# The first splits of the mixed outputs queued in pairs behind attention units, the mask put into the decays, and a query tile with pages of its own

## The chip, the cores and the metric

The kernel runs on one core of a Trainium2 chip. The metric is device time in microseconds of one execution, as the median of several runs. A profile is one execution with every instruction recorded; its span goes from the first to the last instruction. Engines: PE (TensorE matmuls), PEld (its weight loads), DVE (VectorE), ACT (ScalarE), POOL (GpSimd), SP (the queue that issues most DMAs).

## The reference

One encoder layer on a sequence of 1024 with width 1024. Both mixers read the same normalised input; their outputs are joined, projected and added, and a feed-forward layer follows.

```python
def reference(x, ...):
    u = rms_norm(h, mix_norm_gain)
    aq, ak, av, dqkv, dgate, da, db = split(u @ w_in)
    o_att = rms_norm(chunked_rel_attention(aq, ak, av, ...), att_out_gain)  # 8 heads of 64, 576 keys a chunk
    dq, dk, dv = split(silu(causal_short_conv(dqkv)))
    o_dn = gated_delta_rule(dq, dk, dv, log_decay, beta)                    # 4 heads of 128, chunks in turn
    o_dn = rms_norm(o_dn, dn_out_gain) * silu(dgate)
    h = h + concat([o_att, o_dn]) @ w_out
    z = rms_norm(h, ffn_norm_gain) @ w_ff1
    return h + square(relu(z)) @ w_ff2
# in gated_delta_rule, for each chunk:
    l_mask = where(tril, exp(where(tril, diff, 0.0)), 0.0)       # diff: differences of summed log decays
    attn_intra = where(tril, (q @ k.T) * l_mask, 0.0)
```

## The kernel before, in words

All matrix products of the projections are exact to nearly float32: each operand is split into a high part (a cast to a shorter float32 form, by ACT, line 142) and a low part (the difference, by DVE or POOL, line 145), and three products are summed (`mm3`, line 158).

The stages, in order of time: the projections of the input (to about 347 us), then attention and the delta rule together (to about 584 us), then the output projection (to about 676 us), then the feed-forward layer to the end.

Attention works in units (`attention`, line 698): two groups `g` of four heads, eight tiles `t` of 128 queries, two pairs `pp` of heads, 32 units in all. `start` loads a tile's query page by two DMAs on SP, 64 partitions each (line 760), into one of two pages "x", which the tiles use in turn; high and low part of the queries are the two halves (`m`) of the page. `score` makes the products (lines 778 and 779), adds a bias and takes a minimum on DVE (lines 794 and 803; the bias pages `biasn` of the first group lie in the two pages "on") and the exponential on ACT (lines 809 and 812). `value` transposes the result on PE (lines 830 and 841), copies it out of PSUM (`t_tb` by ACT, line 833; `t_ta` of the first head of the pair by ACT, line 846, of the second by DVE, line 844) and multiplies it with the values (line 851). Units of a tile `t` below 2 have no `t_ta`, so there are 24 such copies on each engine. `finish` and `turn` scale the tile, take the sum of its squares on ACT (line 879) and write it transposed into `mixa`.

The delta rule goes over eight chunks of 128 rows (`delta_all`, line 679). `delta_state` carries the state; `delta_out`, one chunk later, forms the decays `Lt` (`decay`, line 462: two POOL products, two matmuls, an exponential on ACT), multiplies the scores with them on DVE (line 654), masks the product on POOL (line 655), multiplies it with the new values on PE (`c_po`), adds, takes a sum of squares (`sumsq`), turns it into a factor by a row of small POOL instructions (`c_ss`, `c_v`, `c_y`, `c_t`, `c_r`) and scales the output with it on POOL (line 664). `delta_fin` transposes the output (`c_tpo`) and writes it into `mixd`.

`out_proj` (line 917) splits the mixed outputs of each half of the rows (`mixed(hf)`, line 929) into `mh` and `ml`, eight parts each, and multiplies them with the output weights (`op`). Only the first half's `mixed(0)` is under an order constraint (line 969).

The order in which each engine issues its instructions is fixed when the program is built: a planner goes through a simulated time with costs of its own, and takes on each engine the earliest written of the instructions that are then ready and have a page free. On the chip each engine issues in that order, and an instruction that must wait holds up those behind it. `tc.issue_after(ins)` puts what is written inside it, as far as it runs on the engine of `ins`, behind `ins` in that engine's order; it makes nothing wait for `ins` to end.

Of the kernel before, what the change touches and what calls it, by code (L numbers as in the profile page):

```python
# [8 lines left out]
F32 = mybir.dt.float32  # L9
F32R = mybir.dt.float32r  # L10
AF = mybir.ActivationFunctionType
ALU = mybir.AluOpType
AX = mybir.AxisListType

P = 128
SEQ = 1024
DM = 1024
# [17 lines left out]
N_W = 10  # L35
ORDER = "OSMOSMFSOMOSMSL"
LATE = 2
RS = "a"
NV = 6
WV = 2.5  # L40
# [3 lines left out]
def hymba_kernel(  # L44
# [20 lines left out]
    nc = tc.nc  # L65
# [16 lines left out]
    def page(tag, name, dt=F32, w=512):  # L82
        return pools[tag].tile([P, w], dt, tag=tag, name=name, bufs=slots[tag])
# [8 lines left out]
    def part(t, i):  # L92
        return t[:, i * 512:(i + 1) * 512]
# [7 lines left out]
    def b4(ap):  # L101
        return ap.rearrange("p (a b) -> p a b", a=4)
# [3 lines left out]
    tri_u = mpool.tile([P, P], F32, name="tri_u")  # L106
# [3 lines left out]
    for t, pat, cm, base in ((tri_u, 1, -1, 0), (tri_s, -1, 1, -1)):  # L110
        nc.gpsimd.affine_select(
            out=t, in_=ones, pattern=[[pat, P]], compare_op=ALU.is_ge,
# [27 lines left out]
    def split(src, hi, lo, hi_eng, lo_eng):  # L140
        if hi_eng is nc.scalar:
            nc.scalar.copy(hi, src)  # L142
        else:
            hi_eng.tensor_copy(hi, src)
        lo_eng.tensor_tensor(lo, src, hi.bitcast(F32), ALU.subtract)  # L145
# [79 lines left out]
    q_dr = dram.tile([NT, 64, 2, 2, 512], F32, name="q_dr")  # L225
# [218 lines left out]
    def bc_mask(m):  # L444
        return m.unsqueeze(1).broadcast_to([P, 4, P])

    def bc_row(s):
        return s.unsqueeze(2).broadcast_to([P, 4, P])
# [13 lines left out]
    def decay(tag, n, ab, h4, msk, lhs, eng):  # L462

        g1 = page(tag, n + "g1", F32R)
        g2 = page(tag, n + "g2", F32R)
        eng.tensor_tensor(b4(g1), bc_mask(msk), bc_row(ab["gh"][:, h4]), ALU.mult)
        nc.gpsimd.tensor_tensor(b4(g2), bc_mask(msk), bc_row(ab["gl"][:, h4]), ALU.mult)
        dp = bank(ps_d, n + "d")
        nc.tensor.matmul(dp, lhs, g1, start=True, stop=False)
        nc.tensor.matmul(dp, lhs, g2, start=False, stop=True)  # L470
        L = page(tag, n)
        nc.scalar.activation(L, dp, AF.Exp)
        return L

    last_delta = [None]

    def sumsq(sq, st, tp, n):
        last_delta[0] = nc.scalar.activation(sq, tp, AF.Square).ins
        ss = small(st, n + "_ss", 4)
        nc.vector.tensor_reduce(ss, b4(sq), AX.X, ALU.add)  # L480
        return ss
# [153 lines left out]
    def delta_out(c, ab, kTs, D):  # L635
        n = f"c{c}"
        T = "wh" if c + 1 < NT else "cv"
        h4 = slice(4 * c, 4 * c + 4)
        kT = kTs[c]
        dq, dg, vn, o = D.pop(c)  # L640
        Lt = decay(T, n + "_Lt", ab, h4, tri_u, tri_sr, nc.gpsimd)
        yield 450
        tp = bank(ps_d, n + "_tpq")
        four_t(tp, head(dq))
        nq = rsqrt("c", sumsq(tp, "c", tp, n + "q"), 4, 1.0, EPS, n + "q")
        qs = small("c", n + "_qs", 4)
        nc.gpsimd.tensor_scalar(qs, nq, P ** -0.5, None, ALU.mult)
        q2 = small("c", n + "_q2", 4)
        nc.gpsimd.tensor_tensor(q2, qs, qs, ALU.mult)
        yield 500  # L650
        mp = bank(ps_d, n + "_mt")
        four(mp, lambda h, hs: kT[:, hs], lambda h, hs: dq[:, hs])
        att = page(T, n + "_att")
        nc.vector.tensor_tensor(att, mp, Lt, ALU.mult)
        nc.gpsimd.tensor_tensor(b4(att), b4(att), bc_mask(tri_u), ALU.mult)
        yield 900
        po = bank(ps_d, n + "_po")
        four(po, lambda h, hs: att[:, hs], lambda h, hs: vn[:, hs])
        nc.vector.tensor_tensor(o, o, po, ALU.add)
        ss = sumsq(po, "c", o, n)  # L660
        nc.gpsimd.tensor_tensor(ss, ss, q2, ALU.mult)
        f = rsqrt("c", ss, 4, 1.0 / P, EPS, n)
        nc.gpsimd.tensor_tensor(f, f, qs, ALU.mult)
        nc.gpsimd.tensor_tensor(b4(o), b4(o), bc_row(f), ALU.mult)
        D[c] = o, dg
        yield 900

# [30 lines left out]
    def attention(after):  # L698
# [54 lines left out]
        def start(g, t):  # L753
            n = f"t{g}{t}"
            T = dict(n=n, k0=max(0, t - 4))
            T["kb"] = max(0, t - 1)
            q = page("x", n + "_q", F32R, w=DM)
            qf = q.bitcast(F32)
            for r0 in (0, 64):
                nc.sync.dma_start(out=qf[r0:r0 + 64].rearrange("p (m c) -> p m c", m=2), in_=q_dr[t, :, :, g, :])  # L760
            T["q"] = q
            T["sums"] = small("t", n + "_sum", 8)
            T["nm"] = small("t", n + "_nm", 8)
            T["s"] = {}
            tiles[g, t] = T

        def product(g, T, i, bk, off, ka, kb):

            q = T["q"]
            cost = 0  # L770
            for hf in range(2):
                a, b = max(ka, 4 * hf), min(kb, 4 * hf + 4)
                if a >= b:
                    continue
                k = keys[g][hf][i]
                o = bk[:, off + (a - ka) * P:off + (b - ka) * P]
                c = slice((a - 4 * hf) * P, (b - 4 * hf) * P)
                nc.tensor.matmul(o, q[:, i * P:(i + 1) * P], k[:, c], start=True, stop=False)  # L778
                nc.tensor.matmul(o, q[:, 512 + i * P:512 + (i + 1) * P], k[:, c], start=False, stop=True)  # L779
                cost += max(214, (b - a) * 107)  # L780
            return cost

# [34 lines left out]
        def value(g, t, pp):  # L817
            T = tiles[g, t]
            n, k0, kb = (T[k] for k in ("n", "k0", "kb"))
            na, nb = kb - k0, t + 1 - kb  # L820
            if pp == 0:
                T["po"] = bank(ps_o, n + "_o")
            po = T["po"]
            sa, sb = T["s"].pop(pp)
            T["spare"] = sb
            tp = bank(ps_t, f"{n}_tpb{pp}")
            for e in range(2):
                for j in range(nb):
                    c = e * 256 + 256 - (nb - j) * P
                    nc.tensor.transpose(tp[:, c:c + P], sb[:, c:c + P], ident)  # L830
            tb = page("raw", f"{n}_tb{pp}", w=516)
            w3 = [t_[:, 0:512].rearrange("p (a b) -> p a b", a=2)[:, :, 256 - nb * P:256] for t_ in (tb, tp)]
            nc.scalar.copy(*w3)
            ta = [None, None]
            if na:
                for e in range(2):
                    i = 2 * pp + e
                    tp = bank(ps_t, f"{n}_tpa{i}")
                    for j in range(na):
                        js = slice(j * P, (j + 1) * P)  # L840
                        nc.tensor.transpose(tp[:, js], sa[e][:, js], ident)  # L841
                    ta[e] = page("u", f"{n}_ta{i}")
                    if e:
                        nc.vector.tensor_copy(ta[e][:, 0:na * P], tp[:, 0:na * P])  # L844
                    else:
                        nc.scalar.copy(ta[e][:, 0:na * P], tp[:, 0:na * P])
            for j in range(na + nb):
                for e in range(2):
                    h = 4 * g + 2 * pp + e
                    c = j * P if j < na else e * 256 + 256 - (na + nb - j) * P  # L850
                    nc.tensor.matmul(po[64 * e:64 * e + 64, pp * P:(pp + 1) * P], vt[k0 + j][:, 64 * h:64 * h + 64],  # L851
                                     (ta[e] if j < na else tb)[:, c:c + P], start=(j == 0), stop=(j == na + nb - 1))
            return (na + nb) * 650
# [42 lines left out]
        for i in range(len(units) + lag + late):  # L896
            if i < len(units):
                g, t, pp = units[i]
# [8 lines left out]
            if lag <= i < len(units) + lag:  # L907
                g, t, pp = units[i - lag]
# [3 lines left out]
            if i >= lag + late:  # L912
                g, t, pp = units[i - lag - late]
# [3 lines left out]
    def out_proj():  # L917


        order = (4, 5, 6, 7, 0, 1, 2, 3)  # L920
        w, parts, R = [], [], {}
# [7 lines left out]
        def mixed(hf):  # L929
            parts.append([None] * NKT)  # L930
            low = [quarter(f"ml1{b}", F32R) for b in range(2)] if hf else None
            for k in order:
                src = part(mix[hf][k // 4], k % 4)
                hi = page("u" if hf else ("pp", "cv")[k // 4], f"mh{hf}{k}", F32R)
                lo = part(low[k // 4], k % 4) if hf else page("dk", f"ml{hf}{k}", F32R)
                split(src, hi, lo, nc.scalar, nc.vector)
                parts[hf][k] = hi, lo

        def rows(j, hf, acc):
# [26 lines left out]
            nc.sync.dma_start(out=r2_dr[:, hf * TH:(hf + 1) * TH], in_=acc)  # L966

        weights(0)
        with tc.issue_after(last_delta[0]):
            mixed(0)  # L970
        acc = rows(0, 0, None)
        weights(1)
        acc = rows(1, 0, acc)
# [376 lines left out]
```

## Time and profile before

| | |
|---|---|
| runs | 1312.46 us median of 3 (1310.26 to 1317.01) |
| the profiled execution | 1309.98 us, span 1307.9 us |
| mean granted clock of PE | 0.988 of full speed |
| busy | PE 97%, PEld 80%, DVE 72%, ACT 42%, POOL 23% |
| matmuls | 6658 |

Matmuls are pipelined and their ends are modelled, so that a busy PE is not PE at its peak. A bracket at the end of a line of a timeline is idle time of that engine just before the instruction, and what ended it. "x4" counts instructions that were merged into one line; the second column is then their time together.

### The profile page before, as it was taken

How to read it: one execution, taken by the hardware profiler on the slowest of the kernel's cores; microseconds unless marked ns; L12 is line 12 of the kernel's file. 1: busy time of each engine (PE TensorE's matmuls, PEld its weight loads, DVE VectorE, ACT ScalarE, POOL GpSimd, SP SyncE). 2: the span in 40 equal slices, each digit the busy share in tenths (PEclk: the TensorE clock that was granted, in tenths of full speed). 3: DMA queues.
4: the chain of work that ended last, by engine and by line, in shares of the span. 5: the costliest groups of instructions: out<-in, count | busy, mean ns of one | idle time of the engine just before them, and what ended most of it. 6: DMA issues, size and time to landing. Idle time of an engine off the chain costs nothing.

```text
span 1307.9 us, 17991 instructions
## 1 busy us (share of the span) xinstructions
PE 1265.2 (97%) x6658; PEld 1041.5 (80%) x6658; DVE 936.2 (72%) x1395; ACT 553.0 (42%) x918; POOL 301.8 (23%) x507
## 2 busy tenths in 40 slices
PE   8999999999999998979998999999998999999997
PEld 6778878788888777858776888888887888888886
DVE  7899978554056565853639756776669897897997
ACT  7233232233266563754335444444456443333330
POOL 4426552543033364533310000000000000000034
PEclk9999999999999999989998999999999999999999
DMA  7214254665573532114341323323379523322002
GB/s 219 70 45 142 94 157 123 137 161 155 193 225 111 153 94 74 56 46 165 117 153 61 111 100 121 104 92 102 109 249 353 169 86 113 129 82 97 15 33 96
DMA packets 129255, 160.63 MB, mean 123 GB/s; under 512 B 22800, under 2 KB 71952, under 8 KB 128656
## 3 DMA queue, kind: packets, MB, share of 16 engines
q1 hardware_dynamic: 111760, 138.51, 34.1%
q10 hardware_dynamic: 17408, 20.98, 4.7%
q8 instruction: 52, 0.85, 0.3%
q14 instruction: 35, 0.29, 0.1%
HBM read 111.75 MB, written 47.71 MB: 122 GB/s over the span
## 4 chain that ended last, share of the span: by engine, by line
PE 82%; DVE 10%; DMA 3%; issue 2%; POOL 1%; ACT 1%; POOLq 1%; SPq 0%; ACTq 0%; DVEq 0%
PE q L1051 21%; PE p L1128 20%; PE op L163 5%; PE av_ps L163 3%; PE aq_ps L163 3%; PE dk_ps L299 3%; PE t_o L851 3%; PE g_ps L163 3%; PE ak_ps L163 2%; PE dv_ps L163 2%; PE dq_ps L163 2%; PE t_tpb L830 1%; PE t_tpa L841 1%; PE t_sb L778 1%; DMA t_q<-q_dr 1%
## 5 line engine op out<-in xcount | busy, mean ns | idle before, releaser
L1197 POOL TENSOR_TENSOR y<-y,y 128x1024 f32<-128x1024 f32 x6 | 19.4, 3250 | 600.5 <-DVE y L1193 581.6
L794 DVE CUSTOM_DVE_ANT_0 t_pb<-t_sb,biasn 128x256 f32<-128x256 f32 (+1 forms) x64 | 25.7, 403 | 56.8 <-PE t_sb L779 31.2
L1193 DVE TENSOR_TENSOR y<-y,p 128x1024 f32<-128x1024 f32 x46 | 55.3, 1219 | 6.3 <-PE p L1128 5.4
L163 PE MATMUL op<-mh,wo_h 128*128 128x512 f32 x128 | 50.3, 393 | 0.6 <-ACT wo_h L142 0.3
L163 PE MATMUL op<-ml,wo_h 128*128 128x512 f32 x128 | 50.5, 394 | 0.0
L163 PE MATMUL op<-mh,wo_l 128*128 128x512 f32 x128 | 48.3, 391 | 0.0
L809 ACT ACTIVATE t_pb<-t_pb,t_nm 128x256 f32<-128x256 f32 (+1 forms) x64 | 31.7, 495 | 23.1 <-DVE t_nm L803 15.0
L948 DVE TENSOR_TENSOR h<-op,op_x 128x512 f32<-128x512 f32 x16 | 10.8, 688 | 29.7 <-PE op L163 29.7
L851 PE MATMUL t_o<-t_ta,vt 128*64 128x128 f32 x240 | 29.7, 299 | 1.8 <-DVE t_ta L844 1.1
L955 POOL TENSOR_TENSOR op_q<-op_q 128x512 f32<-128x512 f32 x14 | 19.6, 1399 | 48.2 <-ACT op_q L954 48.0
L803 DVE CUSTOM_DVE_ANT_0 t_pa<-t_sa,biaso,t_nm 128x384 f32<-128x384 f32 (+2 forms) x48 | 26.3, 549 | 5.5 <-PE t_sa L779 3.3
L163 PEld LDWEIGHTS op<-mh,wo_h 128*128 128x128 f32 x128 | 24.0, 188 | 6.8 <-ACT wo_h L142 0.7
L163 PEld LDWEIGHTS op<-mh,wo_l 128*128 128x128 f32 x128 | 24.0, 188 | 5.4 <-issue 0.4
L163 PEld LDWEIGHTS op<-ml,wo_h 128*128 128x128 f32 x128 | 24.0, 188 | 5.1 <-issue 0.2
L299 PE MATMUL dk_ps<-uh,wdk_h 128*128 128x512 f32 x56 | 21.7, 413 | 5.5 <-ACT uh L180 5.5
L778 PE MATMUL t_sb<-ks,t_q 128*128 128x256 f32 (+1 forms) x72 | 23.2, 333 | 3.7 <-DMA t_q<-q_dr 3.7
L812 ACT ACTIVATE t_pa<-t_pa,t_nm 128x384 f32<-128x384 f32 (+2 forms) x48 | 26.5, 552 | 0.1
L841 PE MATMUL t_tpa<-ident,t_pa 128*128 128x128 f32 x120 | 21.9, 288 | 4.5 <-ACT t_on L879 3.3
L163 PE MATMUL g_ps<-uh,wg_l 128*128 128x512 f32 x64 | 25.3, 398 | 0.5 <-POOL wg_l L145 0.5
L163 PE MATMUL dv_ps<-ul,wdv_h 128*128 128x512 f32 x64 | 25.5, 398 | 0.0
L851 PEld LDWEIGHTS t_o<-t_ta,vt 128*64 128x64 f32 x240 | 17.9, 143 | 9.5 <-issue 1.9
L163 PE MATMUL dq_ps<-uh,wdq_h 128*128 128x512 f32 x64 | 25.4, 396 | 0.0
(1101 smaller groups left out, 4429.7 us busy)
## 6 DMA issues: line engine op xcount, KB each, us to landing
wa<-in_w_ff_dram SPq DMA_DIRECT2D x32, 512.0 KB
a<-in_w_ff_dram SPq DMA_DIRECT2D x32, 512.0 KB
b<-f_dr SPq DMA_DIRECT2D x32, 512.0 KB
t_q<-q_dr SPq DMA_DIRECT2D x32, 256.0 KB
f_dr<-yy ACTq DMA_DIRECT2D x16, 512.0 KB
f_dr<-zz ACTq DMA_DIRECT2D x12, 512.0 KB
xt<-in_x_t_dram SPq DMA_DIRECT2D x16, 256.0 KB
ks<-k_dr SPq DMA_DIRECT2D x16, 256.0 KB
```

The lines of the kernel that those rows point to most:

```text
L163: nc.tensor.matmul(ps, a, b, start=(i == 0), stop=(i == n - 1))
L299: nc.tensor.matmul(ps[ct], a[:, s], b, start=(k + m == 0), stop=(k == NKT - 1 and m == 2))
L778: nc.tensor.matmul(o, q[:, i * P:(i + 1) * P], k[:, c], start=True, stop=False)
L794: nc.vector.tensor_tensor_reduce(sb[:, c], bk[:, c], new[g][pp][:, c], -1.0, 3.0e38, ALU.add, ALU.min, nm[:, 4 + i:5 + i])
L803: nc.vector.tensor_tensor_reduce(sa[e][:, 0:wa], bk[:, 0:wa], old[g][i][:, 384 - wa:384], -1.0, nm[:, 4 + i:5 + i], ALU.add, ALU.min, nm[: ...
L809: nc.scalar.activation(sb[:, c], sb[:, c], AF.Exp, bias=m, scale=-1.0, accum_out=T["sums"][:, 4 + i:5 + i])
L812: nc.scalar.activation(sa[e][:, 0:wa], sa[e][:, 0:wa], AF.Exp, bias=m, scale=-1.0, accum_out=T["sums"][:, i:i + 1])
L841: nc.tensor.transpose(tp[:, js], sa[e][:, js], ident)
L851: nc.tensor.matmul(po[64 * e:64 * e + 64, pp * P:(pp + 1) * P], vt[k0 + j][:, 64 * h:64 * h + 64], (ta[e] if j < na else tb)[:, c:c + P], ...
L1051: nc.tensor.matmul(part(ps, q), l[:, s], r, start=(k + m == 0), stop=(k == 3 and m == 2))
L1128: nc.tensor.matmul(part(ps[q // 2], q % 2), l[:, s], part(r, k), start=(i + k + m == 0), stop=(i + k + m == 4))
L1193: nc.vector.tensor_tensor(y[i][m], y[i][m], ps[m], op)
```

## The change

Four edits in the stage of attention and delta rule.

1. The splits of `mixed(0)` were all queued on ACT behind the last square of the delta rule. Now they are queued in four pairs, in the order 4, 5 / 6, 7 / 0, 1 / 2, 3 of the parts, behind the `t_ta` copies of the fifth, fourth, third and second unit from the end: the casts behind ACT's copy, the subtractions behind DVE's.
2. The mask is applied by POOL to the decays `Lt`, right after their exponential, and no longer to `att`.
3. The scaling of the chunk's output runs on DVE, no longer on POOL.
4. The query tile (1, 1) has two pages "on" of its own, one for each part, loaded by four DMAs; the other tiles use the two pages "x" in turn as before. The tiles behind it thereby change places in that turn.

```diff
+SPREAD = 5
...
-    last_delta = [None]
+    turned = [[], []]
 
     def sumsq(sq, st, tp, n):
-        last_delta[0] = nc.scalar.activation(sq, tp, AF.Square).ins
+        nc.scalar.activation(sq, tp, AF.Square)
...
         Lt = decay(T, n + "_Lt", ab, h4, tri_u, tri_sr, nc.gpsimd)
+        nc.gpsimd.tensor_tensor(b4(Lt), b4(Lt), bc_mask(tri_u), ALU.mult)
...
         nc.vector.tensor_tensor(att, mp, Lt, ALU.mult)
-        nc.gpsimd.tensor_tensor(b4(att), b4(att), bc_mask(tri_u), ALU.mult)
...
-        nc.gpsimd.tensor_tensor(b4(o), b4(o), bc_row(f), ALU.mult)
+        nc.vector.tensor_tensor(b4(o), b4(o), bc_row(f), ALU.mult)
...
-            q = page("x", n + "_q", F32R, w=DM)
...
+            if (g, t) == (1, 1):
+                T["q"] = [page("on", f"{n}_q{m}", F32R) for m in range(2)]
+                for r0 in (0, 64):
+                    for m in range(2):
+                        nc.sync.dma_start(out=T["q"][m].bitcast(F32)[r0:r0 + 64], in_=q_dr[t, :, m, g, :])
+            else:
+                q = page("x", n + "_q", F32R, w=DM)
...
+                T["q"] = [part(q, m) for m in range(2)]
...
-                        nc.vector.tensor_copy(ta[e][:, 0:na * P], tp[:, 0:na * P])
+                        turned[1].append(nc.vector.tensor_copy(ta[e][:, 0:na * P], tp[:, 0:na * P]).ins)
                     else:
-                        nc.scalar.copy(ta[e][:, 0:na * P], tp[:, 0:na * P])
+                        turned[0].append(nc.scalar.copy(ta[e][:, 0:na * P], tp[:, 0:na * P]).ins)
...
-            for k in order:
+            for j, k in enumerate(order):
...
-                split(src, hi, lo, nc.scalar, nc.vector)
+                with ExitStack() as queue:
+                    if not hf:
+                        for copies in turned:
+                            queue.enter_context(tc.issue_after(copies[j // 2 - SPREAD]))
+                    split(src, hi, lo, nc.scalar, nc.vector)
...
-        with tc.issue_after(last_delta[0]):
-            mixed(0)
+        mixed(0)
```

## Rows read from the trace of the kernel before

**Rows 1.** By stage: busy of PE, PEld, DVE, ACT, POOL; PEclk, DMA share, GB/s.
```profile
490.00:506.00 16.00, 12.75 (x108) 11.19 (x106) 7.87 (x20) 4.96 (x13) 9.23 (x24) 0.89 0.34 99
506.00:552.00 46.00, 44.24 (x412) 38.72 (x412) 34.05 (x97) 27.73 (x77) 24.74 (x62) 1.00 0.16 47
552.00:584.00 32.00, 24.17 (x186) 18.28 (x183) 19.89 (x47) 18.47 (x49) 10.79 (x24) 0.89 0.11 34
584.00:676.00 92.00, 88.68 (x391) 71.83 (x389) 36.92 (x43) 35.90 (x59) 28.88 (x26) 1.00 0.40 135
```

**Rows 2.** Waits of PE, 340 to 575 us: total us, times, longest.
```profile
PE t_sb L778 <- DMA t_q<-q_dr: 3.7, 2, 2.6
PE t_tpa L841 <- ACT t_on L879: 3.0, 1, 3.0
PE c_po L453 <- POOL c_att L655: 2.0, 1, 2.0
```

**Rows 3.** Timeline, tail: start us, us, engine, line, instruction, idle before.
```profile
555.76 2.17 ACT L142 CAST mh<-mixd 128x512 fp32r<-128x512 f32 x4
...
556.53 2.49 DVE L145 TENSOR_TENSOR ml<-mixd,mh 128x512 fp32r<-128x512 f32 x4
556.76 0.51 POOL L661 TENSOR_TENSOR c_ss<-c_ss,c_q 128x4 f32<-128x4 f32 x1 [4.11 <-DVE c_ss L480]
...
559.65 0.90 PE L841 MATMUL t_tpa<-ident,t_pa 128*128 128x128 f32 x3 [2.99 <-ACT t_on L879]
...
560.61 0.20 POOL L663 TENSOR_TENSOR c_r<-c_r,c_qs 128x4 f32<-128x4 f32 x1
...
562.26 1.12 PE L457 MATMUL c_tpo<-ident,c_o 128*128 128x128 f32 x4 [1.71 <-POOL c_o L664]
```

**Rows 4.** Granted clock after two pauses (columns as in rows 1).
```profile
498.00:500.00 2.00, 2.00 (x10) 2.00 (x11) 0.10 (x1) 0.00 (x0) 0.00 (x0) 0.53 0.00 0
562.00:564.00 2.00, 1.74 (x8) 1.41 (x8) 0.58 (x1) 0.00 (x0) 1.49 (x6) 0.50 0.00 0
```

**Rows 5.** Timeline around the masked product of a middle chunk.
```profile
495.67 0.68 DVE L654 TENSOR_TENSOR c_att<-c_mt,c_Lt 128x512 f32<-128x512 f32 x1
...
496.61 1.26 POOL L655 TENSOR_TENSOR c_att<-c_att,tri_u 128x512 f32<-128x512 f32 x1
...
497.92 1.94 PE L453 MATMUL c_po<-c_vn,c_att 128*128 128x128 f32 x8 [2.01 <-POOL c_att L655]
```

**Rows 6.** Timeline, the same product in another chunk.
```profile
538.64 1.05 PE L453 MATMUL c_po<-c_vn,c_att 128*128 128x128 f32 x8
```

**Rows 7.** Timeline, first and last small POOL instruction of a factor.
```profile
502.08 0.20 POOL L661 TENSOR_TENSOR c_ss<-c_ss,c_q 128x4 f32<-128x4 f32 x1 [4.22 <-DVE c_ss L480]
...
504.87 0.20 POOL L663 TENSOR_TENSOR c_r<-c_r,c_qs 128x4 f32<-128x4 f32 x1
```

**Rows 8.** Timeline, loads of query tiles and products that waited for them.
```profile
441.93 1.18 SPq L760 DMA_DIRECT2D t_q<-q_dr  x2
...
448.63 0.39 PE L778 MATMUL t_sb<-ks,t_q 128*128 128x256 f32 x1 [2.59 <-DMA t_q<-q_dr]
...
458.80 2.48 SPq L760 DMA_DIRECT2D t_q<-q_dr  x4
...
463.89 0.36 PE L778 MATMUL t_sb<-ks,t_q 128*128 128x256 f32 x1 [1.14 <-DMA t_q<-q_dr]
```

**Rows 9.** Two tiles by line: ns min/median/max, first and last start.
```profile
L659 DVE TENSOR_TENSOR c_o<-c_o,c_po x8: 682/688/689, 395.6 to 554.1; 128x512 f32<-128x512 f32 x8
...
L664 POOL TENSOR_TENSOR c_o<-c_o,c_r x8: 1041/1042/1042, 404.0 to 561.2; 128x512 f32<-128x512 f32 x8
...
L881 DVE TENSOR_SCALAR t_on<-t_on,t_r x8: 480/486/1466, 472.4 to 593.8; 128x512 f32<-128x512 f32 x8
```

**Rows 10.** Timeline, ACT's copies of the fifth and second-last unit.
```profile
548.01 0.46 ACT L846 COPY t_ta<-t_tpa 128x384 f32<-128x384 f32 x1
...
576.83 0.47 ACT L846 COPY t_ta<-t_tpa 128x384 f32<-128x384 f32 x1
```

More of the change, by code (lines that the diff above doesn't have):

```diff
@@ L756, in start @@
             T["kb"] = max(0, t - 1)
-            q = page("x", n + "_q", F32R, w=DM)
[L758 to L761, printed above, removed]
+            if (g, t) == (1, 1):
[5 more added lines that the diff above has]
+                q = page("x", n + "_q", F32R, w=DM)
+                qf = q.bitcast(F32)
+                for r0 in (0, 64):
+                    nc.sync.dma_start(out=qf[r0:r0 + 64].rearrange("p (m c) -> p m c", m=2), in_=q_dr[t, :, :, g, :])
+                T["q"] = [part(q, m) for m in range(2)]
             T["sums"] = small("t", n + "_sum", 8)
@@ L777, in product @@
                 c = slice((a - 4 * hf) * P, (b - 4 * hf) * P)
-                nc.tensor.matmul(o, q[:, i * P:(i + 1) * P], k[:, c], start=True, stop=False)
-                nc.tensor.matmul(o, q[:, 512 + i * P:512 + (i + 1) * P], k[:, c], start=False, stop=True)
+                for m in range(2):
+                    nc.tensor.matmul(o, q[m][:, i * P:(i + 1) * P], k[:, c], start=(m == 0), stop=(m == 1))
                 cost += max(214, (b - a) * 107)
```

## The prediction, made before the result was known

> **What bounds the kernel now.** I read the table of stages first. From 584 us on the output projection keeps TensorE busy 88.68 of 92 us, so whatever ends sooner before it moves the rest of the kernel forward and nothing after it can add to that. The change lies between 360 and 584 us, where attention units and delta chunks share one TensorE queue that is written out beforehand and issued in order. There the share falls in two places: 12.75 of 16 us between 490 and 506, and 24.17 of 32 us between 552 and 584, both at a mean granted clock of 0.89 [rows 1]. Second I asked who waits on TensorE: the long single waits are for a query tile's DMA (3.7 us in two waits), for ScalarE's sum over an attention output (3.0) and for GpSimd's masked `att` (2.0) [rows 2]. Third come the timelines around them.
>
> At the tail, ScalarE runs four casts of `mixed(0)` in one piece from 555.76 (2.17 us) and two pairs more after them, with the sum that TensorE waits for in between; TensorE stands 2.99 us until 559.65. VectorE subtracts at the same time (2.49 us for four). TensorE then waits another 1.71 us, for the scaled output of the last chunk, and only at 562.26 may it transpose it [rows 3]. After each long pause the granted clock is at the lower of its two levels, 1.2 GHz: 0.50 in 562 to 564, and 0.53 mean in 498 to 500 [rows 4].
>
> In the middle, VectorE writes `att` until 496.35 (495.67 + 0.68), GpSimd masks it from 496.61 for 1.26 us, and TensorE starts the product at 497.92, after 2.01 us of nothing, at the low clock: 1.94 us for the eight [rows 5] that take 1.05 at full clock [rows 6].
>
> **The change part by part.**
>
> *Mask.* Per chunk a GpSimd product leaves the path from `att` to `c_po` and an equal one comes behind the exponential of the decays. At 497.92 the product could start at about 496.4, 1.5 us sooner, the pause shrinks to about 0.5 us, and if the clock holds the eight cost 1.05 instead of 1.94: 1.5 + 0.9 = 2.4 us [rows 5, 6]. The list of waits has it once in eight chunks [rows 2], so I count it once. The bounds are 0 (VectorE is late for another reason) and 3.3 (the product behind it is spared its slow clock too). The new product sits beside the score units, several us ahead of its reader; without that cover it costs the same 1.26 us, in the same place. I take a gain of 2.4.
>
> *Scale of the output on VectorE.* GpSimd's takes 1.04 us; a VectorE product of the same size takes 0.69 [rows 9]. In the last chunk this lies on the path: from `c_ss` at 556.76 to the last small product at 560.61 + 0.20 the small GpSimd instructions need 4.05 us [rows 3], beside VectorE's subtractions; the same instructions of an earlier chunk, with VectorE idle or in other work, need 502.08 to 505.07, 2.99 [rows 7]. So with the subtractions spread the factor is ready at 556.76 + 2.99 = 559.75, the scaled output 0.1 + 0.69 later at 560.5, 1.7 us before 562.26. For the other seven chunks the row moves 0.69 us each to VectorE, which is busy 34.05 of 46 us between 506 and 552 [rows 1]: nothing if it fills VectorE's pauses, at most 7 × 0.69 = 4.8 us. I take nothing, because GpSimd is left 1.04 us shorter each time.
>
> *Spread of the first splits.* The arithmetic is the same, eight casts and eight subtractions; only the places move. Pair 0 goes behind the copies of the fifth unit from the end, at 548.01, pairs 1 to 3 behind the fourth, third and second, the last at 576.83 [rows 10]. The first effect: ScalarE reaches the sum right after the square, and the wait of 2.99 us at 559.65 goes. What is late next is the scaled output, at 560.5. So of 2.99 + 1.71 = 4.7 us of pause, 1.7 goes surely; the rest goes where the written order puts other attention work there. There is some: three more units' copies follow up to 576.83 [rows 10], and neither they nor the products that read them need that output. If the pause goes, so does its slow clock. The mean of 0.89 in 552 to 584 is 0.11 × 32 / 0.5 = 7 us at half rate [rows 1], about 4 of them with work, so 2 us. The bounds are 1.7 and 6.7; I take two thirds of the upper, 4.5, since the work to fill it with exists but its order is unknown. The second effect is a cost: a pair is 2.17 / 2 = 1.1 us of ScalarE and 2.49 / 2 = 1.2 us of VectorE [rows 3], and pairs 1 to 3 now stand between the last units, where TensorE waits on just these two engines. Bounds 0 and 4 × 2.3 = 9.3 us; I take one ScalarE pair on the path, 1.1, because both engines still pause over a third of that stretch [rows 1].
>
> *Query tile (1, 1).* Today its DMAs leave at 441.93, when the tile that held its page is done, and TensorE waits 2.59 us for them; the next two tiles leave together at 458.80 and cost 1.14 us [rows 8]. With its own pages the tile (1, 2) has the page at 441.93, 17 us ahead: the second wait goes, 1.1 us. The tile (1, 1) itself waits for two bias pages instead, the first free a unit earlier, the second at about the same time as the old page. So SP issues four half DMAs instead of two, and tile (1, 2)'s 512 KB may stand in front of the second half. The first wait lands between 0 and 2.59 + 2 us; I take it as unchanged. What is queued behind these DMAs on SP (the next chunk's loads) goes out some us later, with readers over ten us away.
>
> **The sum.** −2.4 − 4.5 + 1.1 − 1.1 = −6.9 us. The profiled execution took 1309.98 us (span 1307.9), so 1303.1; the median of the runs shown is 1312.46, 2.5 above it, and I forecast 1305.6 there. All this assumes the order stays as it is elsewhere, but the order is planned anew from the first chunk on, which can shift small waits either way by a few us.
>
> **The rivals.** *All pauses go.* The tail gives its full 6.7, the mask 3.3, both query waits 3.7, and no pair is on the path: −13.7, 1298.8. For it: the pauses have separate causes and each is addressed. Against: the second half of tile (1, 1) still leaves when it did.
>
> *The wait changes hands.* At the tail TensorE reaches the transpose of the last chunk early and stands there until 560.5: −1.7, the clock still falls, one pair costs 2.3, the mask gives 1.5: −0.9 and the query tile's gain is used up by the half that comes late, 1311.6. For it: the queue is in order and that transpose stood right behind the pause. Against: the planner sees it ready late.
>
> *Slower: pairs in the last units' way.* All four pairs stand ahead of an exponential or a copy that TensorE needs, +9.3, the tail's pause stays, only the mask's 2.4 is gained: 1319.4. It decides from the second pair on (2 × 2.3 eats what the tail gives). For it: the stretch from 564 to 584 is a relay of ScalarE, VectorE and TensorE. Against: the work queued there comes after its own unit's copies.
>
> *The port.* GpSimd and VectorE hold each other up: an output scaling of 0.48 us on VectorE took up to 1.47 [rows 9], and `c_ss` 0.51 instead of 0.20 beside the subtractions [rows 3, 7]. If all eight moved scalings lose 1.0 us each on the path, the gain turns into +1.1: 1313.6. The median of that row, 0.49, says that most meet nobody. The Trainium skill states the rule for this (SBUF — State Buffer, "Who interferes with whom"): a VectorE instruction with two SBUF inputs and a GpSimd instruction that reads SBUF exclude one another for a whole instruction, and the one issued second blocks. By that rule moving work between these two can pay nothing; the slowed rows agree with it, their medians show how seldom it strikes here.
>
> **How the numbers follow.** Forecast 0.43 (its own range 1301 to 1310); all pauses go 0.17; the wait changes hands 0.22; slower by the pairs 0.13; the port 0.05. A measurement of this kernel can tell about 0.5%, 6.6 us: faster is below 1305.9, slower above 1319.0. Faster takes somewhat over half of the forecast's, all of the first rival's and a few of the rest: 0.48. Slower takes most of the fourth case and new waits from the new order: 0.13. The rest, 0.39, is the same. The range 1295 to 1317 leaves out the better end of the first rival (0.07) and most of the slower one (0.11).
>
> **What would show it.** Right: no wait of `t_tpa` for the sum `t_on` above 1 us, no `c_po` behind a GpSimd mask, a second query wait of zero, and the projection's first complete bank 5 to 8 us before 584 with its length unchanged. Wrong on the spread: TensorE pauses over 3 us before the last `c_tpo`, or casts `mh` ahead of a copy or exponential that TensorE waits for. Wrong on the query tile: a wait for `t_q` over 3 us near 449. The whole is wrong if the projection begins as before or later, or if the time from there to the end grows.

## The result: 1297.6 us, about twice the gain forecast

The changed kernel takes 1297.57 us (median of 4 runs, 1296.61 to 1298.39); the kernel before took 1312.4 on the same chip (4 runs). The ratio is 0.9882, 95% interval 0.9855 to 0.9909, so 14.8 us are gained. The forecast was 1305.6, a gain of 6.9; the time lies inside the stated range of 1295 to 1317.

The profiled execution took 1296.61 us, its span is 1294.9 and its mean granted clock 0.994. Two rows of each kernel say where the gain arose: the projection's products with the low part of the weights, which begin with its first complete bank, and the delta rule's last writes (ns min/median/max, first and last start). First the kernel before:

```profile
L163 PE MATMUL op<-mh,wo_l x128: 387/389/501, 583.5 to 672.6; 128*128 128x512 f32 x128
...
L675 DVE SCALAR_TENSOR_TENSOR mixd<-c_tpo,dng,c_jg x8: 748/750/751, 413.6 to 563.4; 128x512 f32<-128x512 f32 x8
```

and the changed one:

```profile
L164 PE MATMUL op<-mh,wo_l x128: 387/389/500, 571.8 to 660.9; 128*128 128x512 f32 x128
...
L676 DVE SCALAR_TENSOR_TENSOR mixd<-c_tpo,dng,c_jg x8: 740/744/751, 413.6 to 547.7; 128x512 f32<-128x512 f32 x8
```

The projection starts 11.7 us sooner and is as long as before (89.1 us in both). The other 1.3 us of the span come after it, where nothing was changed: there the two profiled executions differ in the clock (a mean of 0.77 from 705 to 720 us before, 0.89 from 694 to 709 after, 1.8 us in those 15), so this part is not put down to the change. The delta rule starts its first write at the same time and its last one 15.7 us sooner.

To see at which places TensorE lost less, take idle time plus (1 − clock) × length. Three windows, in the columns of [rows 1], before:

```profile
430.00:470.00 40.00, 36.22 (x354) 30.66 (x353) 20.49 (x68) 22.36 (x66) 16.32 (x40) 0.96 0.42 115
490.00:510.00 20.00, 15.46 (x144) 13.49 (x142) 10.03 (x25) 6.33 (x17) 10.42 (x26) 0.91 0.27 80
540.00:583.00 43.00, 35.17 (x288) 28.19 (x288) 29.66 (x76) 25.87 (x69) 18.68 (x47) 0.92 0.13 37
```

and after, the last again up to where the projection starts:

```profile
430.00:470.00 40.00, 38.34 (x386) 32.99 (x386) 23.89 (x76) 23.88 (x72) 16.31 (x46) 1.00 0.46 122
490.00:510.00 20.00, 18.46 (x178) 15.94 (x177) 12.56 (x33) 9.38 (x25) 9.71 (x25) 1.00 0.37 99
540.00:572.00 32.00, 27.09 (x230) 21.47 (x230) 24.05 (x65) 21.67 (x58) 8.77 (x24) 0.95 0.11 34
```

| place | lost before: idle + clock | lost after | given back | forecast there |
|---|---|---|---|---|
| query tiles, 430 to 470 | 3.8 + 1.6 | 1.7 + 0 | 3.7 | 1.1 |
| masked chunk, 490 to 510 | 4.5 + 1.8 | 1.5 + 0 | 4.8 | 2.4 |
| tail, from 540 | 7.8 + 3.4 | 4.9 + 1.6 | 4.7 | 3.4 |

The sum, 13.2, is an upper reading (idle time at a low clock counts twice) and stands beside 11.7 measured. All three places give more than forecast, and 5.2 of the 13.2 is the clock alone. The waits of [rows 2] are gone or short; in the list of TensorE's waits from 340 to 575 us now stand first:

```profile
PE t_tpa L848 <- ACT t_tb L840: 3.0, 2, 2.2
PE t_sb L786 <- DMA t_q<-q_dr: 1.2, 1, 1.2
```

The timelines that answer to [rows 3, 5, 8], from 439 us to the tail:

```profile
439.02 1.11 SPq L762 DMA_DIRECT2D t_q<-q_dr  x2
...
445.48 0.45 SPq L762 DMA_DIRECT2D t_q<-q_dr  x1
...
446.61 0.45 SPq L762 DMA_DIRECT2D t_q<-q_dr  x1
...
450.81 0.36 PE L786 MATMUL t_sb<-ks,t_q 128*128 128x256 f32 x1 [1.22 <-DMA t_q<-q_dr]
...
480.59 1.27 POOL L643 TENSOR_TENSOR c_Lt<-c_Lt,tri_u 128x512 f32<-128x512 f32 x1
...
488.95 0.69 DVE L656 TENSOR_TENSOR c_att<-c_mt,c_Lt 128x512 f32<-128x512 f32 x1
...
488.95 0.43 PE L858 MATMUL t_o<-t_ta,vt 128*64 128x128 f32 x2
...
489.32 0.51 PE L786 MATMUL t_sa<-ks,t_q 128*128 128x256 f32 x2
...
490.70 1.16 PE L454 MATMUL c_po<-c_vn,c_att 128*128 128x128 f32 x8
...
542.01 0.20 POOL L662 TENSOR_TENSOR c_ss<-c_ss,c_q 128x4 f32<-128x4 f32 x1 [1.81 <-DVE c_ss L481]
...
546.31 0.66 PE L458 MATMUL c_tpo<-ident,c_o 128*128 128x128 f32 x4
...
548.83 0.60 ACT L886 ACTIVATE t_on<-t_on 128x512 f32<-128x512 f32 x1 [0.80 <-DVE t_on L881]
...
551.84 1.14 ACT L143 CAST mh<-mixd 128x512 fp32r<-128x512 f32 x2
...
559.34 0.94 SPq L1039 DMA_DIRECT2D wa<-in_w_ff_dram  x2
...
563.28 1.04 ACT L143 CAST q_0a_h<-wa 128x1024 fp32r<-128x1024 f32 x1 [0.90 <-issue]
564.23 0.58 ACT L840 COPY t_tb<-t_tpb 128x512 f32<-128x512 f32 x1
...
564.86 0.55 PE L848 MATMUL t_tpa<-ident,t_pa 128*128 128x128 f32 x3 [2.25 <-ACT t_tb L840]
```

The mask runs 7 us ahead of its reader, and the masked product starts without a wait, behind attention products (`t_o`, `t_sa`) that now stand in front of it. ScalarE's sum at 548.83 has no cast in front of it, and the last chunk's output is transposed at 546.31 without a wait, 16 us sooner than in [rows 3]. The last four lines are the longest wait that is left, and a new one: a cast of the next stage's weights (`q_0a_h`) now stands in ScalarE's queue ahead of the copy `t_tb`; its load left only at 559.34, ScalarE stood 0.90 us before it and cast for 1.04, and TensorE stood 2.25 us for the copy behind. The profile names no releaser there ("issue"); that it is the load is read from what the cast reads.

### The profile page after: what moved, and what is told of

It is laid out like the page before. It is cut to its first block, busy times and chain, and to the rows that moved or that the text cites. A ratio compares the mean times of both kernels' runs of the same rounds, so it can differ in the third digit from the quotient of the medians.

```text
span 1294.9 us, 17977 instructions
## 1 busy us (share of the span) xinstructions
PE 1259.5 (97%) x6658; PEld 1037.4 (80%) x6658; DVE 941.6 (73%) x1403; ACT 551.9 (43%) x918; POOL 292.4 (23%) x499
## 4 chain that ended last, share of the span: by engine, by line
PE 72%; DVE 8%; DMA 2%; POOL 2%; ACT 2%; issue 1%; POOLq 1%; SPq 0%; ACTq 0%; DVEq 0%
PE q L1061 21%; PE p L1138 20%; PE op L164 5%; PE av_ps L164 3%; PE aq_ps L164 3%; PE g_ps L164 3%; PE t_o L858 3%; PE ak_ps L164 2%; PE t_sb L786 1%; PE t_sa L786 1%; PE t_tpb L837 1%; PE t_tpa L848 1%; PE c_pv L454 1%; PE c_pS L454 1%; PE c_po L454 1%
## 5 line engine op out<-in xcount | busy, mean ns | idle before, releaser
L786 PE MATMUL t_sb<-ks,t_q 128*128 128x256 f32 (+1 forms) x144 | 30.4, 307 | 1.5 <-DMA t_q<-q_dr 1.2
L786 PE MATMUL t_sa<-ks,t_q 128*128 128x256 f32 (+2 forms) x128 | 25.6, 310 | 0.3 <-DVE t_nm L801 0.3
L164 PE MATMUL aq_ps<-waq_h,uh 128*128 128x512 f32 x64 | 25.3, 401 | 0.0
```

What stands on the lines that cost most here:

```text
L164: nc.tensor.matmul(ps, a, b, start=(i == 0), stop=(i == n - 1))
L786: nc.tensor.matmul(o, q[m][:, i * P:(i + 1) * P], k[:, c], start=(m == 0), stop=(m == 1))
```

## The experiments

Two theories were held against each other. By the first (theory A in the expectations), which the prediction used, each edit gives back the pause at its own place, and the gains add up. By the second (theory B) the edits are also inputs of the planner: any of them makes it lay out the whole order of attention and delta rule anew, and much of the gain is that order. The experiments undo one edit of the changed kernel, or make one alone. A side question was whether the mask's place shortens the chain of the delta rule. Medians are compared with the kernel before on the same chip (1311.0 to 1311.4).

### One edit undone

Against the changed kernel:

```diff
# no_query
-            if (g, t) == (1, 1):
+            if False:
# no_mask
-        nc.gpsimd.tensor_tensor(b4(Lt), b4(Lt), bc_mask(tri_u), ALU.mult)
...
+        nc.gpsimd.tensor_tensor(b4(att), b4(att), bc_mask(tri_u), ALU.mult)
# no_scale
-        nc.vector.tensor_tensor(b4(o), b4(o), bc_row(f), ALU.mult)
+        nc.gpsimd.tensor_tensor(b4(o), b4(o), bc_row(f), ALU.mult)
# no_spread (last_delta is the last square, as before)
-                    if not hf:
+                    if False:
...
-        mixed(0)
+        with tc.issue_after(last_delta[0]):
+            mixed(0)
```

> All four edits but the query tile's: tile (1, 1) takes its turn on the two pages again. Theory A (each edit removes the pauses of its own place): the two waits of TensorE for query tiles come back, 3.7 us against 1.2, with a stretch of low clock behind them, and nothing else moves: about 3.5 us slower than the changed kernel, 1301. Theory B (the order planned anew is what counts, and any edit reshuffles it): the time moves by up to 6 us either way and the waits that appear lie elsewhere. Theory C (only the spread of the splits matters): within 1.5 us of 1297.6.

> All four edits but the mask's: GpSimd masks the product again. Theory A: the pause before the product of a middle chunk comes back with its low clock, 490 to 510 us loses about 4.7 us against the changed kernel: 1302. Theory B: up to 6 us either way, with no wait for GpSimd's masked product above 1 us. Theory C: within 1.5 us of 1297.6.

> All four edits but the scale's: GpSimd scales the chunk's output again, 1.04 us instead of 0.69. Theory A: about 0.4 us on the path of the last chunk, at most 1.7: 1298 to 1299. Theory B: up to 6 us either way. Theory C: within 1.5 us of 1297.6.

> All four edits but the spread: the eight splits of the first half stand behind the last square of the delta rule again. Theory A: the burst of casts comes back and with it a wait of TensorE for ScalarE's sum of about 3 us at the tail: 3 to 4.5 us slower than the changed kernel, 1301 to 1302. Theory B: up to 6 us either way, without such a wait. Theory C: most of the gain goes, 1308 or more.

| undone | median, us | ratio to before (interval) | against 1297.57 |
|---|---|---|---|
| query tile | 1301.76 | 0.9914 (0.9886 to 0.9942) | +4.2 |
| mask | 1301.21 | 0.9913 (0.9882 to 0.9944) | +3.6 |
| scale | 1295.41 | 0.9873 (0.9846 to 0.9900) | −2.2 |
| spread | 1299.08 | 0.9901 (0.9874 to 0.9928) | +1.5 |

The parts sum to 7.1 of 14.8 us. The changed kernel was not run beside these four: taken by the ratios instead, the four differences are +4.2, +4.1, −1.2 and +2.5, and each of the four intervals overlaps the changed kernel's (0.9855 to 0.9909). The mask stands out, since no run with it undone comes down to the ten of the changed kernel (at most 1299.11, with those of the second occasion below), and so does the query tile but for one run (1298.91); the signs of the other two are not shown. Without the query tile's own pages the second wait for query DMAs is back at its place, with the next two tiles leaving together again as in [rows 8]:

```profile
459.52 2.46 SPq L767 DMA_DIRECT2D t_q<-q_dr  x4
...
464.43 0.47 PE L786 MATMUL t_sb<-ks,t_q 128*128 128x256 f32 x2 [1.92 <-DMA t_q<-q_dr]
```

The list of waits has 3.2 us for query tiles (the first wait, 1.25, is as long as in the changed kernel), and 460 to 470 runs at a granted clock of 0.83. This edit acts where it stands.

The mask does not. With it back on `att`, no wait for GpSimd's mask returned in 490 to 510: the planner had put other work there. Two windows of that kernel:

```profile
490.00:510.00 20.00, 17.54 (x167) 14.69 (x165) 12.86 (x34) 9.26 (x27) 11.03 (x26) 1.00 0.35 93
540.00:577.00 37.00, 29.76 (x248) 24.23 (x247) 26.57 (x66) 21.67 (x58) 13.62 (x35) 0.91 0.09 29
```

The loss is at the tail, 7.2 us idle and 3.3 of clock, and most of it is one pause:

```profile
559.38 0.95 SPq L1039 DMA_DIRECT2D wa<-in_w_ff_dram  x2
...
566.05 1.04 ACT L143 CAST q_0a_h<-wa 128x1024 fp32r<-128x1024 f32 x1 [4.74 <-issue]
...
568.72 0.90 PE L848 MATMUL t_tpa<-ident,t_pa 128*128 128x128 f32 x3 [6.02 <-ACT t_tb L840]
```

It is the wait for the next stage's weights again, with the load issued at the same time and the cast 2.8 us later than in the changed kernel. No edit touches it. This is one profile, of a run of 1304.2 us, the longest of its four (the others 1300.7 to 1301.6), so its length is not that of all runs. The delta rule's last write is at 561.6 instead of 547.7.

Without the spread the eight casts run in one piece again but for one copy, from 541.1 to 545.9, since the last square of the delta rule comes some 14 us sooner in that order, and no attention sum is late there. The burst costs little once it is early.

The kernel without the mask edit is also the scale alone (further below) with the query tile and the spread added, and with 1301.21 it is not faster than the scale alone (1298.86, on another occasion): in that order the two edits bring nothing that can be seen.

### One edit alone

Against the kernel before:

```diff
# only_mask
+        nc.gpsimd.tensor_tensor(b4(Lt), b4(Lt), bc_mask(tri_u), ALU.mult)
...
-        nc.gpsimd.tensor_tensor(b4(att), b4(att), bc_mask(tri_u), ALU.mult)
# only_query
+            if (g, t) == (1, 1):
+                T["q"] = [page("on", f"{n}_q{m}", F32R) for m in range(2)]
...
# only_spread
+                            queue.enter_context(tc.issue_after(copies[j // 2 - SPREAD]))
...
-        with tc.issue_after(last_delta[0]):
-            mixed(0)
+        mixed(0)
# drop_mask
-        nc.gpsimd.tensor_tensor(b4(att), b4(att), bc_mask(tri_u), ALU.mult)
```

The last one leaves the mask out altogether, so its delta rule does not compute the reference's.

> The kernel before with the mask edit alone. Theory D (the mask's 1.3 us stood in every chunk's chain; without it the delta rule ends well before the last attention units, and the tail's pauses go with it): the last chunk's mixd is written near 550 instead of 563 us, the projection begins 5 to 8 us sooner, 1304 +- 2. Theory A (each edit clears its own place): only 490 to 510 us gets better, 1311 - 3 = 1308. Theory B (any new plan): no pattern, 1305 to 1317.

> The kernel before with the query tile's pages alone. Theories A and D: the two waits for query tiles shrink from 3.8 us to about 1.3 and the low clock behind them goes, 430 to 470 us loses 3.5 to 4.2 us, 1307. The tail keeps its pauses. Theory B: no pattern, 1305 to 1317.

> The kernel before with the splits in pairs alone. Theory D: the last chunk's output still comes at about 560, so TensorE stands before its transpose instead of behind the casts; at most 2 us gained, 1309 to 1311. Theory A: the wait of 3 us for ScalarE goes with its low clock, 1306 to 1307. Theory B: no pattern.

> The kernel before without any mask in the delta rule's output: the product on GpSimd is left out, so the outputs of the delta rule are not the reference's. Theory D: as with the mask in the decays, since only its place in the chain counted: within 2 us of that run. A theory E, that the new product behind the exponential costs something on GpSimd: this one is faster by more than 2 us.

| alone | median, us | ratio (interval) | against 1311.38 |
|---|---|---|---|
| mask in the decays | 1305.24 | 0.9953 (0.9936 to 0.9971) | −6.1 |
| query tile | 1306.80 | 0.9969 (0.9954 to 0.9983) | −4.6 |
| spread | 1304.92 | 0.9947 (0.9926 to 0.9969) | −6.5 |
| no mask | 1303.51 | 0.9935 (0.9914 to 0.9957) | −7.9 |

Three edits alone sum to 17.2, more than all four together. The query tile is worth nearly the same alone (4.6) and undone (4.2): alone, too, 430 to 470 runs at a granted clock of 1.00, with 1.9 us idle: the first wait is 1.93 us, the second is gone.

The spread alone is the cleanest look at the tail, since the delta rule there ends as late as before (563.7). Of the kernel with the spread alone:

```profile
554.91 0.42 DVE L881 TENSOR_TENSOR t_on<-t_on,t_tot 128x256 f32<-128x256 f32 x1
...
556.05 0.58 ACT L886 ACTIVATE t_on<-t_on 128x512 f32<-128x512 f32 x1
...
556.81 1.05 PE L848 MATMUL t_tpa<-ident,t_pa 128*128 128x128 f32 x6 [0.18 <-ACT t_on L886]
...
557.77 1.14 ACT L143 CAST mh<-mixd 128x512 fp32r<-128x512 f32 x2
...
562.39 0.66 PE L458 MATMUL c_tpo<-ident,c_o 128*128 128x128 f32 x4
```

```profile
540.00:579.00 39.00, 35.08 (x291) 28.04 (x291) 31.64 (x76) 25.51 (x68) 17.64 (x47) 0.96 0.14 39
```

The sum starts 1.1 us after its input, with no cast before it; the transposes that waited for it until 559.65 now start at 556.81, and those of the scaled output, at 562.39 as before [rows 3], stand behind other work and wait for nothing. Idle time falls from 7.8 to 3.9 us and the clock's loss from 3.4 to 1.6. The pairs between the last units cost nothing that can be seen. The other two places lose as much as before (36.40 of 40 us busy at a clock of 0.96, 15.46 of 20 at 0.91).

The mask alone takes the loss at 490 to 510 from 4.5 + 1.8 to 2.3 + 0, 4.0 us; its delta rule's last write is at 559.5, 3.9 us sooner and not the dozen that a shorter chain was expected to give. Leaving the mask out is 1.7 us better than moving it, less than either scatters: no cost of the product in its new place can be seen.

### The scale alone, and the scale left out

`after_again` is the changed kernel and `no_scale_again` the third of the kernels with one edit undone, once more, now beside each other. The other two:

```diff
# only_scale, against the kernel before
-        nc.gpsimd.tensor_tensor(b4(o), b4(o), bc_row(f), ALU.mult)
+        nc.vector.tensor_tensor(b4(o), b4(o), bc_row(f), ALU.mult)
# free_pairs, against no_scale: the splits are queued behind nothing
-                    if not hf:
+                    if False:
```

> The changed kernel once more, beside the next one on the same chip: 1297 to 1298.

> The changed kernel with the scale left on GpSimd, beside it: if the scale on VectorE costs what its undoing gave (2.2 us), 1295 to 1296 and below every run of the changed kernel but its lowest; if that was the chip, within 1 us of it.

> The kernel before with the scale on VectorE alone. If the prediction's step holds (the last chunk's output comes 0.4 to 1.7 us sooner, and the rest is covered), 1310 to 1311. If VectorE's and GpSimd's instructions hold each other up, or VectorE's queue is the late one, 1313 or more.

> The changed kernel with the scale on GpSimd and no order constraint on the splits of the first half: the planner takes them as soon as their parts and pages are there. If what counted in the spread is only that the casts don't come in one piece behind the last square, within 1.5 us of the kernel with pairs. If the place behind the copies counts, the casts stand earlier in front of exponentials that TensorE waits for, and it is 2 to 6 us slower.

| | median, us | ratio (interval) |
|---|---|---|
| the change, again | 1298.30 | 0.9890 (0.9869 to 0.9911) |
| the change without the scale, again | 1294.94 | 0.9874 (0.9851 to 0.9897) |
| the scale alone | 1298.86 | 0.9901 (0.9879 to 0.9922) |
| without the scale, splits free | 1297.73 | 0.9889 (0.9868 to 0.9909) |

The scale alone missed every expectation: 12.2 us of gain from moving eight products of 1.04 us to an engine where they take 0.69. Alone it does as much as all four edits together, and on top of the other three it gives nothing that can be seen; the medians are 2 to 3 us higher with it. Its trace shows how. The mask is still on `att`, the splits are still behind the last square, the query tile has its old page; yet all three places lose less (the same windows as above):

```profile
430.00:470.00 40.00, 38.11 (x389) 32.85 (x387) 22.98 (x74) 23.02 (x70) 17.07 (x45) 1.00 0.43 124
490.00:510.00 20.00, 17.77 (x167) 14.71 (x166) 12.68 (x34) 9.54 (x28) 10.46 (x26) 1.00 0.34 92
540.00:573.00 33.00, 28.39 (x249) 23.54 (x248) 26.05 (x66) 21.96 (x60) 14.88 (x36) 0.95 0.11 33
```

And this is the masked product that [rows 5] showed, in that kernel:

```profile
489.56 0.69 DVE L656 TENSOR_TENSOR c_att<-c_mt,c_Lt 128x512 f32<-128x512 f32 x1 [0.16 <-PE c_mt L454]
...
490.33 1.28 POOL L657 TENSOR_TENSOR c_att<-c_att,tri_u 128x512 f32<-128x512 f32 x1 [2.42 <-DVE c_att L656]
...
492.86 0.56 PE L787 MATMUL t_sb<-ks,t_q 128*128 128x256 f32 x3
...
493.26 0.99 PE L454 MATMUL c_po<-c_vn,c_att 128*128 128x128 f32 x7
```

The same mask, 1.28 us long, stands between the same two instructions, and costs nothing: the written order has attention products in front of `c_po`, which starts 1.65 us after the mask has ended. The second theory holds for this edit: what pays is the order, not the 0.35 us (eight times that is 2.8).

How far an edit changes the order can be read from the profiles, since they show each engine's instructions in the order in which it issued them. Between 345 and 600 us ScalarE has 388 instructions that write tiles of attention and delta rule, VectorE 428, GpSimd 238. With the query tile alone ScalarE's and GpSimd's stand as before, and on VectorE one changes place. With the spread alone the order is that of before up to about 555 us. With the mask alone ScalarE's order departs at 394 us, with the scale alone at 409. So the first theory holds for the query tile and the spread, whose gains alone come without a new order, and only the mask and the scale bring another order.

The kernel without the scale had the lowest median on both occasions. It is 3.4 us below the changed kernel on the second, with intervals and ranges that overlap (1294.39 to 1297.89 against 1295.37 to 1299.11), so that it is faster is not shown. Two profiles of this one program, of runs of 1297.44 and 1294.39 us, differ in the clock: the tail of the first, then of the second.

```profile
540.00:572.50 32.50, 28.23 (x237) 21.79 (x236) 24.43 (x65) 21.58 (x58) 10.46 (x27) 0.95 0.11 34
```

```profile
540.00:570.00 30.00, 24.95 (x217) 18.89 (x211) 22.48 (x58) 20.75 (x57) 9.81 (x23) 1.00 0.11 36
```

From 430 to 470 the first has a clock of 0.96 and the second 1.00, so the clock's share of a gain at one place can come and go between executions of the same program.

With the splits free in it the casts run from 535.4 and the median rises by 2.8, with ranges that overlap (1295.40 to 1299.05). In the profile the clock of the tail is 0.90, and the wait behind `q_0a_h` is 2.8 us; no pair in front of an exponential is seen to cause it. Its projection starts at 572.8, where the two profiles of the kernel with pairs have 572.5 and 569.9. Whether the place behind the copies counts is not settled.

## Why the prediction was half right

The time is inside the range and below the forecast's own 1301 to 1310. The pauses were named rightly; what each edit does to them was sized for an order that stays, and two of the four edits change it.

**What bounds the kernel.** Right. The projection kept its length and moved forward, by 11.7 us instead of 6.9.

**Mask, 2.4.** The wait of 2.01 us is gone, and no cost of the product in its new place can be seen. But the step from the shorter path to the shorter pause is not shown, since the order changed too. Before, TensorE had only small products between the scores `c_mt` and `c_po`, and the last of them was done 2.01 us before `c_po` started [rows 5]:

```profile
493.91 1.06 PE L453 MATMUL c_mt<-c_jq,kT 128*128 128x128 f32 x8
494.90 0.41 PE L574 MATMUL m_tp<-ident,m_yb 64*64 64x64 f32 x4
495.24 0.67 PE L576 MATMUL m_tp<-m_yb,m_ab 64*64 64x64 f32 x8
```

In the changed kernel attention products stand there as well, and `c_po` starts 1.1 us after `att` is written. Two kernels with the mask still on `att` (the scale alone, and the mask undone) lose the wait too. The term was also mis-sized: the place gave back 4.8 in the changed kernel and 4.0 with the mask alone, above the upper bound of 3.3.

**Scale, nothing.** Wrong as a term of its own, and the step that failed is the assumption behind it: I counted 0.69 us against 1.04 at their places, while "the order stays as it is elsewhere" was only named as a condition of the sum. The order is the larger effect: −12.2 alone, and in company no gain (+2 to +3 by the medians, not clear of noise). The part that I put on the tail's path did not decide anything: from `c_ss` at 542.01 to the transpose at 546.31 it still takes 4.3 us, and nobody waits.

**Spread, 4.5 less 1.1.** Right in its mechanism, which the spread alone shows: the sum is early, and attention work fills the wait for the scaled output, the case that I gave two thirds. It was worth 6.5 alone, near the upper bound of 6.7; the pair on ScalarE, 1.1, did not appear. In the company of the others its 1.5 us is not clear of noise: there the delta rule ends early, and the burst stands where nothing waits for it.

**Query tile, 1.1.** Mis-sized: the place gave 3.7. Of the new page's four DMAs two leave at 439.02, ahead of the old 441.93, and two at 445.48 and 446.61, as late as feared; but "I take it as unchanged" was wrong: the first wait falls from 2.59 to 1.22 us (1.93 with this edit alone), and the low clock behind it goes as well. Its 4.2 to 4.6 us are 2.1 of idle time, 1.6 of clock, and up to 0.9 us that I can't place. "A second query wait of zero" was met: the wait that is left, at 450.81, is the first tile's (33 of VectorE's 64 additions of `biasn` come before it; 32 came before the first wait in the kernel before, and 40 before the second).

**The rivals.** "All pauses go" (1298.8) comes closest to the time, but partly by luck. The query tiles' place gave the 3.7 that it counted (with a wait of 1.22 left and the clock gained), the masked chunk 4.8 where it had 3.3, and the tail 4.7 where it had 6.7. And its reason, that each pause has its own cause and its own edit, does not hold for the scale, which alone lessens all three. The slower rival fell: the pairs stand behind the copies, as at 551.84, and the one wait over 1 us that is left for ScalarE is behind the weights' cast, not behind a pair. That wait is a rival I did not have. The port struck the moved products once in the changed kernel, where one of the eight runs into the new mask:

```profile
458.14 1.28 POOL L643 TENSOR_TENSOR c_Lt<-c_Lt,tri_u 128x512 f32<-128x512 f32 x1 [1.13 <-ACT c_Lt L473]
...
458.21 1.75 DVE L665 TENSOR_TENSOR c_o<-c_o,c_r 128x512 f32<-128x512 f32 x1
```

It takes 1.75 us instead of 0.69 and ends 0.5 us after the mask. The rule of the Trainium skill that the prediction cited (SBUF — State Buffer, "Who interferes with whom") agrees with this pair: the later instruction stands until the earlier one is over. The other seven take 0.68 to 0.73, and with the scale alone, where no mask stands beside the decays, all eight take 0.68 to 0.69: it is a price of single collisions here. Of the two slowed rows that the prediction read by that rule, `c_ss` stood beside subtractions with two SBUF inputs; the scaling `t_on` has one such tensor and a factor for each row, so it is not the case that the rule was cited for, though its slowest (577.56 to 579.03 before) also ended just after a GpSimd product (577.48 to 578.75).

**What stays open.** For the mask and the scale, how much of the gain is the place and how much the new order can't be parted by these runs; the scale's own place explains under 3 us of its 12. Alone the four edits sum to 29.4, together they give 12.7 to 14.8, undone one by one 7.1. A run with the order held fixed and the mask moved in it would tell; it was not tried; nor was a kernel that holds the weights' cast back until the last units' copies are out. Nor is it known why the scale's order is so much better alone: the traces show which pauses it lessens, and that the other edits lessen them too, but not what in the planner's costs brings the order about.

## What to carry to other kernels

Where a planner writes the order, an edit can have two prices: the one at its place, which a trace can tell beforehand, and the one of the new order, which only a run tells; the second was some 9 us or more here, for the scale alone. Compare the order of the instructions in the profiles before and after: two of the four edits left it almost as it was, and their gains could be read at their places. Try each edit alone and each one undone, since gains of edits that clear the same pauses don't add up. When a pause of TensorE goes, count the slow clock behind it as a bound: it may not have been there in another execution.

## What the runs showed of the hardware

A pause of TensorE can cost more than its length, because the granted clock may fall behind it. Before, with TensorE at work for only 1.41 of the 4 us from 446, the next 4 us ran at a granted 0.57 with TensorE busy throughout, 4 × 0.43 = 1.7 us:

```profile
446.00:450.00 4.00, 1.41 (x14) 1.11 (x14) 0.94 (x3) 0.48 (x1) 1.26 (x1) 1.00 0.73 237
450.00:454.00 4.00, 4.00 (x31) 3.16 (x29) 0.51 (x5) 1.56 (x4) 0.00 (x0) 0.57 0.37 101
```

It need not fall. With the query tile alone TensorE stands 1.99 us before the masked product, as long as the 2.01 of [rows 5], but the clock stays at 1.00 and the eight take 1.16 us where they took 1.94:

```profile
495.50 1.16 PE L454 MATMUL c_po<-c_vn,c_att 128*128 128x128 f32 x8 [1.99 <-POOL c_att L657]
```

```profile
498.00:502.00 4.00, 2.91 (x25) 2.24 (x26) 2.01 (x6) 1.06 (x3) 2.39 (x8) 1.00 0.00 0
```

The steps are much the same size each time: places lose 1.6 to 1.8 us of clock (490 to 510 before, the tail after) or twice that (the tail before), or none. The runs of the kernel before scatter with it: from 1307.09 us at a mean granted clock of 0.991 to 1319.11 at 0.980.
